# A causal convolution's tap products moved from VectorE to ScalarE and adding transfers, in a hybrid encoder block

## The chip, the cores and the metric

The kernel runs on one core of one Trainium2 chip. The metric is device microseconds of one execution on that core; three runs of a kernel are timed and the median counts. Engines are named TensorE (PE in the profile), VectorE (DVE), ScalarE (ACT), GpSimd (POOL) and SyncE (SP). SyncE does no arithmetic here and issues nearly all transfers.

## The reference, cut to what matters

One layer of an encoder block, 256 rows of 4096 float32 values, all in float32. A wide input projection gives the parts of two branches: 16 heads of chunked attention, and a convolution module on 2048 channels. The change touches the causal depthwise convolution of the second branch, with 31 taps:

```python
u = a * jax.nn.sigmoid(g)
u = jnp.pad(u, ((0, 0), (CONV_K - 1, 0), (0, 0)))
u = lax.conv_general_dilated(
    u, w_dw[:, None, :], window_strides=(1,), padding='VALID',
    dimension_numbers=('NWC', 'WIO', 'NWC'),
    feature_group_count=CONV_WIDTH) + b_dw
u = jax.nn.silu(layer_norm(u, ln_g, ln_b))
return u @ w_pw + b_pw
```

So for each channel, output row t is the bias plus the sum over k of `w_dw[k]` times `u[t + k - 30]`. What follows it (layer norm, a pointwise product, gates, an output projection, a gated embedding and a last norm) is the same in both kernels.

## The kernel before

Every large product runs on TensorE in three passes: each float32 weight tile `wt` is split into a high part `wh` (a cast on ScalarE, line 204) and a low part `wl` (a subtraction on VectorE, line 205), and each block of activations was split likewise. `wh` and `wl` have three buffers each, `wt` has five. A product covers two column blocks of 512 at once (`mixed_product`) in 16 units of two 128-row blocks. A plain unit takes two `wt` tiles and 24 matmuls of 128x512. A unit with a star in the order strings (`early`, `dense` and so on) uses seven products in place of eight: 21 matmuls, and it also casts two sums of weight blocks, `ua` and `ub` (into `uh` and `ul`). Weights come by transfers of 512 KB that SyncE issues.

The order in time is: input projection of the convolution's `a` and `g` for column blocks 0 and 1 (`glu_conv(0)`, `glu_conv(1)`), then queries and keys, values, attention, `glu_conv(2)`, `glu_conv(3)`, more keys and attention, the layer norm, and so on.

`glu_conv(c)` ends with `uT`, the gated input of 512 channels with channels on partitions: four channel blocks of 128 channels by 256 rows, in one tile 128x4x256. The convolution of these four blocks is then not issued at once. Its instructions go as small closures into a queue `later`, and each unit of the products that follow takes a given number of closures from it (`fill`, by the list `early_fills`: 64 for a product of 16 units). There are 124 closures for one `uT`, in all 496 for the four. A scheduler then decides where each instruction stands on its engine, and it may bring one forward; engines run their instructions in that order.

Before, each closure is one VectorE instruction: `conv_tap` for one channel block and one tap. The first writes `cv` as product plus bias (line 678), the other 30 add one shifted product into `cv` in place (line 682). The layer norm (`layer_norm_swish`) reads all four `cv` tiles after the last of them is done. `cv` lies in the pool `act`, which has eight buffers of 4 KB a partition.

GpSimd has little to do: fills of constants, four times a fill of a part of `bias` for the attention (line 901), and a few tiny powers.

Of the kernel before, what the change touches and what calls it, by code (L numbers as in the profile page):

```python
# [10 lines left out]
F32 = mybir.dt.float32  # L11
F32R = mybir.dt.float32r
AF = mybir.ActivationFunctionType
ALU = mybir.AluOpType
AX = mybir.AxisListType

P = 128
# [8 lines left out]
def hybrid_block(  # L26
# [23 lines left out]
    nc = tc.nc  # L50
    _, T, D = x.shape
# [5 lines left out]
    TAPS = w_dw.shape[1]  # L57
    PAD = TAPS - 1
# [9 lines left out]
    def pool(name, bufs, stack=ctx, side=0, **kw):  # L68
        return stack.enter_context(tc.tile_pool(name=name, bufs=bufs, side=sides[side], **kw))

    cpool = pool("cpool", 1)
    act = pool("act", 8)
# [13 lines left out]
    def tmp_psum():  # L86
        return ps_tmp.tile([P, 512], F32, tag="tmp", name="tmp_ps")
# [92 lines left out]
    later = deque()  # L180
# [300 lines left out]
    def scaled_pair(w, col, apart, order, r, fills, home={}, then=lambda: None, **kw):  # L481

        t, z = [], []

        def on_helpers(helper):
            for dst, src in zip((t, z), sum_tiles(**home)):
                dst.extend(src)
            then()
            nc.scalar.activation(z[0][0], helper["P1"], AF.Identity, scale=r[:, :1])
            helper_sums(helper, z)  # L490
            for h, j in QUARTERS[1:]:
                nc.scalar.activation(z[h][j], z[h][j], AF.Identity, scale=r[:, h : h + 1])

        c = mixed_product(w, col, xT, xS, order, on_helpers, fills=fills, apart=apart, **kw)
        for h, j in QUARTERS:
            stt(
                z[h][j], c[h][j], r[:, h : h + 1], z[h][j],
                ALU.mult, ALU.subtract if j else ALU.add,
            )
        return t  # L500
# [17 lines left out]
    for c in range(0, 4, 2):  # L518
        if c:
            t = upool.tile([P, 4, 2, T], F32R, tag="big", name="big_t", bufs=1)  # L520
        else:
            t = keep.tile([P, 4, 2, T], F32R, tag="comb", name="comb_t")
# [126 lines left out]
    ln_g, ln_b, bdw, ga, gc, gp = (prm[:, a : a + n] for a, (_, n) in zip(at, rows))  # L649
    dw = spool.tile([P, KCW, TAPS], F32, name="dw", bufs=1)  # L650
# [22 lines left out]

    conv = []

    def conv_tap(cv, uT, i, b, k):
        if k == PAD:
            nc.vector.tensor_scalar(
                cv[:, i, :], uT[:, i, :], dw[:, b, k : k + 1], bdw[:, b : b + 1], ALU.mult, ALU.add
            )  # L680
        else:
            nc.vector.scalar_tensor_tensor(  # L682
                cv[:, i, PAD - k :], uT[:, i, : T + k - PAD], dw[:, b, k : k + 1],
                cv[:, i, PAD - k :], ALU.mult, ALU.add,
            )

    def more_combinations(pair):

        if pair in (7, 9):
            c = (pair + 1) // 2  # L690
            xS[2 * c] = act.tile([P, 2, 2, T], F32R, tag="act", name="comb_x"), 0
            later.extendleft(reversed(combinations(c)))

    def glu_conv(c):
        if c == 0:
            sg, gate = scaled_pair(
                w_in0, o_a, o_g - o_a, first, r_x, (1,), begin=first_pairs
            )
        else:
            last = c == CW // NB - 1  # L700
            sg, gate = scaled_pair(
                w_in0, o_a + c * NB, o_g - o_a, early_six if last else early, r_x, early_fills,
                ahead=more_combinations if last else None,
            )
        for h in range(NH):
            nc.scalar.activation(gate[:, h, :], gate[:, h, :], AF.Sigmoid)
            tt(sg[:, h, :], sg[:, h, :], gate[:, h, :], ALU.mult)
        uT = spool.tile([P, 4, T], F32, tag="hd", name="uT", bufs=5)
        for pair in range(2):
            pt = tmp_psum()  # L710
            for i in range(2):
                for h in range(NH):
                    b = 2 * pair + i
                    nc.tensor.transpose(
                        pt[:, i * T + h * P : i * T + (h + 1) * P],
                        sg[:, h, b * P : (b + 1) * P],
                        ident,
                    )
            nc.scalar.copy(
                uT[:, 2 * pair : 2 * pair + 2, :], pt.rearrange("q (i t) -> q i t", t=T)  # L720
            )
        cv = act.tile([P, 4, T], F32, tag="act", name="cv")
        for i in range(4):
            for k in reversed(range(TAPS)):
                later.append(partial(conv_tap, cv, uT, i, 4 * c + i, k))
        conv.append(cv)


# [191 lines left out]
    n_g = H // GH  # L920
    assert n_g == CW // NB == 4
    glu_conv(0)
    glu_conv(1)
    load_bias(0)
    keys(0, early_fills)
    values(0, early, early_fills, home=dict(tag="hd", bufs=5))
    attention(0)
    glu_conv(2)
    glu_conv(3)
    load_bias(1)  # L930
# [139 lines left out]
    for c0 in range(0, D // NB, 2):  # L1070
        for j in range(2):
            hc = act.tile([P, NH, NB], F32, tag="act", name="hc")
            c = c0 + j
# [222 lines left out]
```

## Time and profile before

| | |
|---|---|
| three timed runs | 2048.33, 2048.42, 2051.77 us; median 2048.42 us |
| span of the profiled execution, first to last instruction | 2049.8 us |
| the profiled execution's own time | nothing beside its span is given; the span is 1.4 us above the median of the runs |
| TensorE busy | 2021.3 us, 99% of the span |
| VectorE busy | 1944.7 us, 95% |
| ScalarE busy | 1196.2 us, 58% |
| GpSimd busy | 8.1 us |
| transfers | 412.30 MB, mean 201 GB/s |

The page is one profiled execution. A busy share is an average over stages with different limits, and a matmul counts as busy from its start to its modelled end, so that neighbours overlap. "Idle before" of a group of instructions is the time that its engine stood still just before them, with what ended it.

### The profile page before, as it was taken

The page shows a single profiled execution, that of the slowest core. Times are in us where ns is not written, and L with a number is a line of the kernel's source. Part 1 is how long each engine was busy: PE and PEld are TensorE (multiplying, and loading weights), DVE is VectorE, ACT ScalarE, POOL GpSimd, SP SyncE. Part 2 cuts the span into 40 slices and gives each one's busy share as a digit, 9 for nine tenths or more (in the row PEclk, how much of TensorE's full clock was granted, in tenths as well). Part 3 has the DMA queues.
Part 4 walks back from the last instruction along what each step waited for, and adds up shares of the span by engine and source line. Part 5 has one row for each costly group of instructions (what it writes and reads, how often), then busy time and mean ns, then how long its engine had stood idle before and what let it go on. Part 6 is the DMA issues. An engine that isn't in the chain of part 4 may idle for free.

```text
span 2049.8 us, 26039 instructions
## 1 busy us (share of the span) xinstructions
PE 2021.3 (99%) x9082; PEld 1652.6 (81%) x9082; DVE 1944.7 (95%) x2784; ACT 1196.2 (58%) x1543; POOL 8.1 (0%) x19
## 2 busy tenths in 40 slices
PE   9999999999899999999999999999999999999997
PEld 7888888888678888877888888888888888888876
DVE  7999999989999999988899999999999999999998
ACT  7655545655555544576565656676565666655555
POOL 0000000000000000000000000000000000000000
PEclk9999999999999999999999999999999999999998
DMA  8666666566665665754666566676666656666765
GB/s 284 195 195 205 201 192 203 166 198 184 194 187 170 200 184 184 222 164 168 196 217 206 191 218 196 217 241 208 212 200 202 205 188 209 200 219 206 235 207 178
DMA packets 153662, 412.30 MB, mean 201 GB/s; under 512 B 12974, under 2 KB 16190, under 8 KB 153530
## 3 DMA queue, kind: packets, MB, share of 16 engines
q1 hardware_dynamic: 152880, 409.80, 62.7%
q8 instruction: 71, 1.16, 0.2%
q10 hardware_dynamic: 650, 0.84, 0.1%
q14 instruction: 61, 0.50, 0.1%
HBM read 406.39 MB, written 4.19 MB: 200 GB/s over the span
## 4 chain that ended last, share of the span: by engine, by line
PE 87%; DVE 8%; issue 2%; DMA 1%; ACT 1%; SPq 0%; POOL 0%; POOLq 0%; ACTq 0%; DVEq 0%
PE acc L372 68%; PE acc_P L372 15%; DVE wl L205 3%; DVE cv L682 1%; DVE ul L205 1%; PE tmp_ps L170 1%; DMA wt<-in_w_in_dram 1%; PE acc L218 1%; DVE ub L433 0%; DVE ub L432 0%; PE tmp_ps L835 0%; PE tmp_ps L851 0%; DVE ua L428 0%; PE tmp_ps L869 0%; DVE ua L429 0%
## 5 line engine op out<-in xcount | busy, mean ns | idle before, releaser
L372 PE MATMUL acc<-wh,big_t 128*128 128x512 f32 x4196 | 1296.4, 392 | 4.0 <-DVE wh L563 1.6
L204 ACT CAST wh<-wt 128x1024 fp32r<-128x1024 f32 (+1 forms) x737 | 711.9, 977 | 552.3 <-PE acc L372 408.0
L372 PEld LDWEIGHTS acc<-wh,big_t 128*128 128x128 f32 x4196 | 784.2, 188 | 168.5 <-ACT big_t L156 2.4
L205 DVE TENSOR_TENSOR wl<-wt,wh 128x1024 fp32r<-128x1024 f32 (+1 forms) x737 | 821.0, 1125 | 32.3 <-ACT wh L204 28.9
L372 PE MATMUL acc<-wl,big_t 128*128 128x512 f32 x2098 | 804.0, 391 | 2.0 <-DVE wl L205 1.8
L372 PEld LDWEIGHTS acc<-wl,big_t 128*128 128x128 f32 x2098 | 393.0, 188 | 87.1 <-DVE wl L205 5.7
L682 DVE SCALAR_TENSOR_TENSOR cv<-uT,dw,cv 128x255 f32<-128x255 f32 (+22 forms) x480 | 213.1, 463 | 1.0
L204 ACT CAST uh<-ub 128x1024 fp32r<-128x1024 f32 x130 | 136.9, 1053 | 125.5 <-DVE ub L433 105.1
L204 ACT CAST uh<-ua 128x1024 fp32r<-128x1024 f32 x130 | 137.1, 1054 | 84.9 <-DVE ua L429 79.6
L205 DVE TENSOR_TENSOR ul<-ub,uh 128x1024 fp32r<-128x1024 f32 x130 | 158.7, 1221 | 8.1 <-ACT uh L204 6.9
L372 PE MATMUL acc_P<-uh,big_t 128*128 128x512 f32 x528 | 161.7, 393 | 0.0
L205 DVE TENSOR_TENSOR ul<-ua,uh 128x1024 fp32r<-128x1024 f32 x130 | 158.6, 1220 | 0.9 <-ACT uh L204 0.2
L372 PEld LDWEIGHTS acc_P<-uh,big_t 128*128 128x128 f32 x528 | 97.4, 188 | 24.3 <-ACT uh L204 5.0
L428 DVE TENSOR_TENSOR ua<-wt 128x512 f32<-128x512 f32 x130 | 89.3, 687 | 21.8 <-DMA wt<-in_w_in_dram 15.0
L372 PE MATMUL acc_P<-ul,big_t 128*128 128x512 f32 x264 | 101.1, 394 | 1.0 <-DVE ul L205 1.0
L429 DVE TENSOR_TENSOR ua<-wt 128x512 f32<-128x512 f32 x130 | 89.1, 685 | 2.3 <-DMA wt<-in_w_in_dram 1.3
L433 DVE TENSOR_TENSOR ub<-ub,wt 128x512 f32<-128x512 f32 x130 | 89.1, 686 | 0.8
L432 DVE TENSOR_TENSOR ub<-ua,wt 128x512 f32<-128x512 f32 x130 | 89.1, 685 | 0.3
L372 PE MATMUL acc<-uh,big_t 128*128 128x512 f32 x260 | 80.6, 390 | 0.0
L372 PE MATMUL acc_P<-wh,big_t 128*128 128x512 f32 x260 | 80.6, 389 | 0.0
L372 PE MATMUL acc_P<-uh,comb_t 128*128 128x512 f32 x228 | 70.1, 392 | 0.2
L372 PEld LDWEIGHTS acc_P<-ul,big_t 128*128 128x128 f32 x264 | 49.2, 188 | 15.2 <-DVE ul L205 4.9
(240 smaller groups left out, 1367.4 us busy)
## 6 DMA issues: line engine op xcount, KB each, us to landing
wt<-in_w_in_dram SPq DMA_DIRECT2D x447, 512.0 KB, 4.2
wt<-in_w_out_dram SPq DMA_DIRECT2D x128, 512.0 KB, 4.2
wt<-in_w_ple_gate_dram SPq DMA_DIRECT2D x128, 512.0 KB, 4.1
wt<-in_w_pw_dram SPq DMA_DIRECT2D x32, 512.0 KB, 4.6
hc<-in_x_dram SPq DMA_DIRECT2D x8, 512.0 KB, 5.2
wt<-in_w_ple_dram SPq DMA_DIRECT2D x8, 512.0 KB, 4.7
xin<-in_x_dram SPq DMA_DIRECT2D x7, 512.0 KB, 7.9
out_dram<-hc SPq DMA_DIRECT2D x12, 256.0 KB, 2.4
```

What stands on the lines that cost most here:

```text
L170: nc.tensor.transpose(pt[:, i * T + h * P : i * T + (h + 1) * P], src[:, h, b] if len(src.shape) == 4 else src[:, h, b * P : (b + 1) * P], ...
L204: nc.scalar.copy(wh[:, :kc, :], wt[:, :kc, :]),
L205: nc.vector.tensor_tensor(wl[:, :kc, :], wt[:, :kc, :], wh[:, :kc, :].bitcast(F32), ALU.subtract),
L218: nc.tensor.matmul(acc, a, b[:, k, :], start=kb == 0 and kind == 0, stop=kb == kblocks - 1 and kind == 2,)
L372: nc.tensor.matmul(banks[name], a, b, start=name not in begun, stop=final and ends[name] == n and kind == 2 and not (left and name in "P2 ...
L428: plus(ua[:, 0], w0[:, 0], w0[:, 1])
L429: plus(ua[:, 1], w0[:, 1], w1[:, 1])
L432: plus(ub[:, 0], ua[:, 0], w1[:, 1])
L433: plus(ub[:, 1], ub[:, 0], w1[:, 0])
L682: nc.vector.scalar_tensor_tensor(cv[:, i, PAD - k :], uT[:, i, : T + k - PAD], dw[:, b, k : k + 1], cv[:, i, PAD - k :], ALU.mult, ALU.add,)
```

## The change

Each closure is now a ScalarE instruction. `conv_taps` makes them for one `uT`. Four closures (`start`) write `cv` as product plus bias, for tap 30, which needs no shift. Then, for each of the 30 other taps, four closures (`tap`) write the products of the four channel blocks into one tile `tap` of 128x4x256, shifted; the fourth also has GpSimd issue a transfer of that tile, 512 KB, that adds it into `cv`. Two `tap` tiles alternate, taken from the pool `act`; their first 30 columns, which no product with a shift reaches in full, are set to zero by GpSimd once for each of the two tiles. Taps run from the largest shift (k = 0) to the smallest. VectorE has no part in it any more. The number of closures is the same, 124 for one `uT`.

```diff
-    def conv_tap(cv, uT, i, b, k):
-        if k == PAD:
-            nc.vector.tensor_scalar(
-                cv[:, i, :], uT[:, i, :], dw[:, b, k : k + 1], bdw[:, b : b + 1], ALU.mult, ALU.add
-            )
-        else:
-            nc.vector.scalar_tensor_tensor(
-                cv[:, i, PAD - k :], uT[:, i, : T + k - PAD], dw[:, b, k : k + 1],
-                cv[:, i, PAD - k :], ALU.mult, ALU.add,
-            )
+    def conv_taps(cv, uT, c):
+
+        held = {}
+
+        def start(i):
+            b = 4 * c + i
+            nc.scalar.activation(
+                cv[:, i, :], uT[:, i, :], AF.Identity,
+                scale=dw[:, b, PAD : PAD + 1], bias=bdw[:, b : b + 1],
+            )
+
+        def tap(k, i):
+            if k < 2 and i == 0:
+                held[k] = act.tile([P, 4, T], F32, tag="act", name="tap")
+                nc.gpsimd.memset(held[k][:, :, :PAD], 0.0)
+            t, b = held[k % 2], 4 * c + i
+            nc.scalar.activation(
+                t[:, i, PAD - k :], uT[:, i, : T + k - PAD], AF.Identity,
+                scale=dw[:, b, k : k + 1],
+            )
+            if i == 3:
+                nc.gpsimd.dma_start(cv, t, accum_op=ALU.add)
+
+        yield from (partial(start, i) for i in range(4))
+        yield from (partial(tap, k, i) for k in range(PAD) for i in range(4))
...
         cv = act.tile([P, 4, T], F32, tag="act", name="cv")
-        for i in range(4):
-            for k in reversed(range(TAPS)):
-                later.append(partial(conv_tap, cv, uT, i, 4 * c + i, k))
+        later.extend(conv_taps(cv, uT, c))
         conv.append(cv)
```

In the changed kernel the product of a tap is line 692, its transfer line 697, the zero fill line 690 and the start line 682; lines after it are 13 higher than before.

The order of ScalarE's instructions, in the units of `glu_conv(1)`, before: casts of weights and of their sums stand one behind the other. What a row waits for stands in brackets (DMAHW: a transfer that SyncE issued, DMASW: one that GpSimd issued, PE, DVE, Pool, Activation: that engine).

```order
L204 CAST uh<-ua 128x1024 [waits DVE_49]
L204 CAST wh<-wt 128x1024 [waits DMAHW1_49,PE_49,Activation_49]
L204 CAST wh<-wt 128x1024 [waits DMAHW2_49,PE_49,Activation_49]
L204 CAST wh<-wt 128x1024 [waits DMAHW3_49,PE_49,Activation_49]
L204 CAST uh<-ub 128x1024 [waits DVE_49]
L204 CAST wh<-wt 128x512 [waits DMAHW4_49,PE_49,Activation_49]
L204 CAST wh<-wt 128x1024 [waits DMAHW5_49,DVE_49,PE_49]
```

The same place in the changed kernel, where the products of the taps for rows of 235 to 237 elements stand between the casts:

```order
L204 CAST uh<-ub 128x1024 [waits DVE_49,PE_49]
L692 ACTIVATE tap<-uT,dw 128x235 [waits Activation_49]
L204 CAST wh<-wt 128x1024 [waits DMAHW5_49,PE_49,Activation_49]
L692 ACTIVATE tap<-uT,dw 128x236 [waits DMASW0_49,Activation_49]
L692 ACTIVATE tap<-uT,dw 128x236 [waits Activation_49] x3
L204 CAST wh<-wt 128x1024 [waits DMAHW6_49,PE_49]
L204 CAST wh<-wt 128x1024 [waits DMAHW7_49,PE_49]
L692 ACTIVATE tap<-uT,dw 128x237 [waits DMASW1_49,Activation_49]
L204 CAST uh<-ua 128x1024 [waits DVE_49,PE_49]
```

Behind the casts nothing was taken away; the first product of each tap waits for a transfer of GpSimd, the one that read the same `tap` tile two taps earlier.

GpSimd's order before, from the power for the input norm to the last fill of `bias`:

```order
L139 TENSOR_TENSOR r_x<-r_x,mhalf 128x2 [waits DVE_49,Pool_49]
L901 MEMSET bias 64x4x64 [waits DMAHW3_49]
L901 MEMSET bias 64x4x64 [waits DMAHW5_49,DMAHW3_49,DMAHW7_49,DVE_49,PE_49]
L901 MEMSET bias 64x4x64 [waits DMAHW7_49,DVE_49,Pool_49]
L139 TENSOR_TENSOR r_ln<-r_ln,mhalf 128x2 [waits DVE_49]
L901 MEMSET bias 64x4x64 [waits DMAHW5_49,PE_49]
```

GpSimd's order now, from the 23rd transfer of the first `cv` to the first transfer of the second:

```order
L697 DMA cv<-tap 128x1024 [waits DMASW5_49,Activation_49]
L697 DMA cv<-tap 128x1024 [waits DMASW6_49,Activation_49]
L914 MEMSET bias 64x4x64 [waits DMAHW3_49]
L697 DMA cv<-tap 128x1024 [waits DMASW7_49,Activation_49]
L697 DMA cv<-tap 128x1024 [waits DMASW0_49,Activation_49]
L697 DMA cv<-tap 128x1024 [waits DMASW1_49,Activation_49]
L697 DMA cv<-tap 128x1024 [waits DMASW2_49,Activation_49]
L697 DMA cv<-tap 128x1024 [waits DMASW3_49,Activation_49]
L697 DMA cv<-tap 128x1024 [waits DMASW4_49,Activation_49]
L690 MEMSET tap 128x4x30 [waits DMAHW5_49,PE_49]
L690 MEMSET tap 128x4x30 [waits DMAHW2_49,PE_49]
L697 DMA cv<-tap 128x1024 [waits DMAHW7_49,Activation_49,Pool_49]
```

Each transfer waits for the one before it to land, since both add into the same `cv`, and 120 of them now stand on a queue that held a fill now and then.

## The prediction

> **What bounds the kernel now.** I read the page's head first, then the busy time by stretch, then who waits for whom.
>
> ```profile
> PE 2021.3 (99%) x9082; PEld 1652.6 (81%) x9082; DVE 1944.7 (95%) x2784; ACT 1196.2 (58%) x1543; POOL 8.1 (0%) x19
> ...
> L682 DVE SCALAR_TENSOR_TENSOR cv<-uT,dw,cv 128x255 f32<-128x255 f32 (+22 forms) x480 | 213.1, 463 | 1.0
> ```
>
> TensorE is busy 99% of the span and VectorE 95%; the 480 adding taps are 213 us of VectorE. The question is whether VectorE holds TensorE up where the taps run, 107 to 807 us, and what ScalarE has free there.
>
> ```profile
> core 0: us, PE busy (x) PEld busy (x) DVE busy (x) ACT busy (x) POOL busy (x), PEclk, DMA share, GB/s
> 107.00:807.00 700.00, 692.79 (x3100) 564.31 (x3099) 686.50 (x1089) 364.35 (x434) 0.61 (x2) 1.00 0.62 191
> ```
>
> VectorE is busy 686.5 of 700 us, yet TensorE stands still for only 700 - 692.8 = 7.2 us. So what VectorE does there is nearly all hidden behind matmuls, and 7.2 us is about the most that its relief can bring. ScalarE has 336 us free.
>
> ```profile
> ACT wh L204 <- PE acc L372: 213.3, 129, 4.4
> ```
>
> In the same 700 us ScalarE waits 213 us for TensorE to give back a `wh` buffer: its casts run ahead as far as three buffers allow. This lead is the cushion that a late ScalarE eats first.
>
> **Where the taps now stand.** ScalarE's order keeps the casts of line 204 in nearly the same sequence, so I count casts to place the new work in the old trace. For the first `uT` (block 0) the first tap product stands behind 40 such casts and the last behind 92; for blocks 1 to 3 it is 119 to 168, 200 to 262 and 283 to 331 (counted, up to two off where the stretches below are cut). In the trace of before these casts lie here:
>
> ```profile
> core 0: us, ACT busy (x), PEclk, DMA share, GB/s
> 0.00:106.75 106.75, 39.84 (x40) 1.00 0.73 236
> 106.75:217.22 110.47, 51.09 (x52) 1.00 0.65 201
> 217.22:277.02 59.80, 26.90 (x28) 1.00 0.61 191
> 277.02:387.65 110.62, 48.63 (x49) 1.00 0.62 190
> 387.65:456.56 68.91, 31.59 (x32) 1.00 0.63 197
> 456.56:586.16 129.60, 59.83 (x62) 1.00 0.61 187
> 586.16:635.13 48.97, 21.08 (x21) 1.00 0.60 185
> 635.13:747.18 112.05, 47.21 (x48) 1.00 0.60 184
> ```
>
> So the 120 tap products and 30 transfers of a block do not spread over 700 us: they are packed into four stretches of 110.5, 110.6, 129.6 and 112.1 us, 462.7 us in all, with 49 to 69 us between them in which no tap runs. All engines in these four:
>
> ```profile
> 106.75:217.22 110.47, 110.25 (x487) 89.68 (x486) 109.43 (x175) 56.19 (x61) 0.31 (x1) 1.00 0.65 201
> 277.02:387.65 110.62, 110.62 (x509) 91.28 (x508) 109.88 (x186) 60.31 (x83) 0.00 (x0) 1.00 0.62 190
> 456.56:586.16 129.60, 123.89 (x536) 98.39 (x535) 129.29 (x208) 66.30 (x73) 0.31 (x1) 1.00 0.61 187
> 635.13:747.18 112.05, 111.96 (x519) 91.88 (x518) 109.96 (x189) 58.77 (x82) 0.00 (x0) 1.00 0.60 184
> ```
>
> **VectorE's part removed.** 480 x 0.463 us, and 16 starts. It lay beside TensorE, which stood still 0.2, 0, 5.7 and 0.1 us in these stretches. I take 0 us: the 5.7 us of block 2 vanish into what the stretch becomes below. Both ends: 0 and 7.2 us gained.
>
> **ScalarE's part added.** 480 products and 16 starts. The nearest rows:
>
> ```profile
> L492 ACT ACTIVATE z<-z,r_x 128x512 f32<-128x512 f32 x30 | 20.6, 718 | 12.8 <-DVE z L471 11.1 <-DVE z L473 1.6
> L265 ACT CAST big_t<-comb 128x512 fp32r<-128x512 f32 x20 | 12.0, 616 | 2.6 <-DVE comb L260 2.2 <-issue 0.3
> L804 ACT CAST big_t<-cv 128x256 fp32r<-128x256 f32 x16 | 5.2, 403 | 0.0
> L794 ACT ACTIVATE cv<-cv,prm 128x256 f32<-128x256 f32 x16 | 8.4, 591 | 0.0
> 209.75 2.00 ACT L204 CAST wh<-wt 128x1024 fp32r<-128x1024 f32 x2 [0.70 <-PE acc L372]
> ```
>
> Line 492 is the same operation at 512 columns (scaled by a column, SBUF to SBUF): 0.718 us. The two casts give 616 - 403 = 213 ns for 256 columns, so a product of 256 columns takes 0.505 us and of the mean 240.5 columns 0.49 us. Two casts in a row take 2.00 us together, not 2 x 1.05, so instructions in a row overlap by some 0.1 us, and a product costs 0.40 to 0.49 us. A start is like line 794, 0.59 us. Per block: 120 x 0.40 to 0.49 = 48 to 59 us, plus 2.4. With the 56 to 66 us that ScalarE has there already it comes to 107 to 118, 111 to 122, 117 to 128 and 109 to 120 us, against 110.5, 110.6, 129.6 and 112.1: just full. I take it as hidden; at the upper end blocks 0, 1 and 3 run over by 7, 11 and 8 us.
>
> **The transfers.** 120 of them, 512 KB each. Each waits for the one before it in the same `cv`; the first product of tap k waits for the transfer of tap k - 2; behind this product stand the casts that TensorE needs. So a block takes at least 28 transfers in a row (those of taps 0 to 27) plus the first tap's and the last tap's products, 8 x 0.45 = 3.6 us, and the cushion gives something back: two `wh` tiles ahead, each of 12 matmuls at 110.62 / 509 = 0.217 us, 5.2 us. With D for one transfer from its issue to the next, a block takes 28 D - 1.6 us, and it is late by that less its stretch. The point from which it counts: D = 112 / 28 = 4.0 us for blocks 0, 1 and 3, and 4.7 for block 2.
>
> No adding transfer, none from GpSimd and none from SBUF to SBUF is in the trace. The nearest rows, size and time from issue to landing:
>
> ```profile
> wt<-in_w_in_dram SPq DMA_DIRECT2D x447, 512.0 KB, 4.2
> xin<-in_x_dram SPq DMA_DIRECT2D x7, 512.0 KB, 7.9
> gin_rows<-in_norm_in_g_dram SPq DMA_DIRECT2D x1, 16.0 KB, 2.0
> ...
> q1 hardware_dynamic: 152880, 409.80, 62.7%
> ```
>
> A plain load of this size, beside the other loads, takes 4.2 us; one of 16 KB, which moves nearly nothing, 2.0. So 2.0 is fixed and 2.2 is data. An adding transfer must read two blocks, `tap` and `cv`, and write one. Below, D is the plain 4.2 us; above, twice all of it, 8.4, close to the slowest row of the size, 7.9. I take the fixed part once and the data twice: D = 2.0 + 4.4 = 6.4 us. It is an estimate, and the whole sum hangs on it.
>
> The Trainium skill, page "DMA: Bandwidth & Descriptors", section "Anatomy of one DMA — SWDGE (gpsimd) path", gives a transfer that GpSimd issues 2.0 us plus its bytes over 436 GB/s: for 512 KB an estimate of 3.2 us, under 4.0, so that by it the transfers stay hidden and the time stays near 2048. The trace does not agree for SyncE's loads, 4.2 us beside other traffic, and shows nothing of GpSimd's.
>
> The sum: a block takes 28 x 6.4 - 1.6 = 177.6 us, four 710.4; less 462.7 is 247.7 us. By D = 4.2 a block takes 116.0: late by 5.5, 5.4, 0 and 3.9, +15 us. By 8.4, 233.6 x 4 - 462.7 = +472 us.
>
> Are the 16 transfer engines enough? 409.8 MB took 62.7% of 2049.8 us, so 512 KB take 1.64 us of all of them. Doubled, 120 take 394 us; the weights take 0.62 x 462.7 = 287. Together 681 of 710 us: it is the row of landings that ends a stretch, narrowly, and the loads will land later than 4.2 us.
>
> GpSimd's own: eight zero fills beside the four fills of `bias`, each 0.3 us, on an engine that is idle. The first fill of `bias` now stands behind 24 transfers; the attention that reads it has its exponentials behind tap 24 of block 1, a whole stretch later. If it were not covered, attention 0 would wait for block 0's transfers, which ScalarE waits for anyway: 0 us.
>
> ```profile
> L901 POOL MEMSET bias<- 64x256 f32 x4 | 1.2, 307 | 790.0 <-DMA bias<-in_rel_table_dram 440.0 <-DVE cv L682 350.0
> ```
>
> Span 2049.8 + 247.7 = 2297.5. The median of the runs is 1.4 us under the profiled span, so I predict 2296 us, 12% slower.
>
> **Rivals.** First, on the other side: an adding transfer goes from issue to issue in under 4.0 us, and ScalarE's products cost 0.40. Then no tap waits, and of the 7.2 us of TensorE's standstill up to all is won: 2041 to 2048 us. For it speaks that `tap` and `cv` need no HBM; against it the 4.2 us of a plain load and the second read.
>
> Second: the transfers are hidden, but ScalarE at 0.49 us is over full. Blocks 0, 1 and 3 run over by 7, 11 and 8 us, less 5.2 of cushion each: 2 + 6 + 3 = 11 us, 2060 us.
>
> Third: the waits slow TensorE's clock. A stretch of 178 us holds 111 us of matmuls, so TensorE stands still 38% of the time, in pieces.
>
> ```profile
> 520.00:530.00 10.00, 5.90 (x24) 3.86 (x23) 10.00 (x17) 5.77 (x7) 0.00 (x0) 1.00 0.39 109
> 2040.00:2045.00 5.00, 0.00 (x0) 0.00 (x0) 2.31 (x6) 2.56 (x4) 0.94 (x1) 0.50 0.48 179
> ```
>
> At 5.9 busy of 10 us the granted clock stayed 1.00; with no matmul in 5 us it was 0.50. At half clock the matmuls of a stretch take twice as long, 925 us for the four, which is +463: 2511 us. The Trainium skill, page "TensorE: Matmul & The Clock Gate", section "Part 1: The HAM clock gate (the "warmup" mystery)", has the clock halve after an idle window of some 3.4 us; by that, pieces of 2 to 3 us leave it full. The two rows agree, so I hold this rival for unlikely.
>
> **How the numbers follow.** Row of transfers with a full clock, D from 4.2 to 8.4 or a little over: 77 in 100. Hidden: 11, of which 5 faster by over 0.2% (about what a measurement of this kernel can tell from no change) and 6 within. ScalarE over full: 4. Clock halved: 8. Slower in all 77 + 4 + 8 = 89. The range reaches from 2070 (D = 4.3: 118.8 a block, late by 8.3, 8.2, 0 and 6.7, +23) to 2520 (D = 8.4), which leaves out the hidden cases, ScalarE alone and the far end of the clock's case, about 2 in 10.
>
> **What would show it.** Right: 120 transfers `cv<-tap` of 512 KB from GpSimd with 6 to 7 us from issue to landing; ScalarE's largest new wait is that of `tap`, line 692, for `cv<-tap`, some 250 us; the four stretches take about 178 us each, TensorE busy near 62% in them, its clock 1.00; VectorE far under 90%; the stretches between and all after 807 us unchanged in length. Wrong, if the transfers land in 4 us or less, if the tap products take other than 0.4 to 0.5 us, if a clock of 0.50 shows in the stretches, or if the loads of `wt`, not the taps, are what TensorE waits for.

## The result and the profile after

The changed kernel takes 2307.09 us (median of 4 runs, 2303.75 to 2309.3) against 2049.09 us for the kernel before: a ratio of 1.1257, 95% interval 1.1243 to 1.127. The profiled execution has a span of 2302.0 us, 252.2 us more than before's. The prediction was 2296 us, with a range of 2070 to 2520.

The head of the page after, the chain that ended last, the transfers' queue, the rows of the new work (busy time and mean ns of one, then the engine's idle time before it and its releasers), and the transfers' size and median time from issue to landing:

```profile
span 2302.0 us, 26473 instructions
...
PE 2114.4 (92%) x9082; PEld 1690.5 (73%) x9082; DVE 1774.2 (77%) x2288; ACT 1382.1 (60%) x2039; POOL 113.7 (5%) x147
...
q0 software_dynamic: 17280, 62.92, 14.9%
...
PE 51%; DMA 13%; issue 4%; DVE 3%; ACT 2%; POOL 0%; ACTq 0%; POOLq 0%; DVEq 0%
...
L692 ACT ACTIVATE tap<-uT,dw 128x226 f32<-128x226 f32 (+14 forms) x480 | 207.9, 487 | 278.8 <-DMA cv<-tap 278.7
...
L697 POOL DMA_DIRECT2D cv<-tap x120 | 104.2, 868 | 829.7 <-ACT tap L692 540.7
...
cv<-tap POOLq DMA_DIRECT2D x120, 512.0 KB, 5.2
```

VectorE's share fell from 95 to 77%, but TensorE's fell too, from 99 to 92%, and transfers now make up 13% of the span in the chain of work that ended last. Where they are seen is the view of one line: the transfers' own instructions, what GpSimd waited for ahead of them, and who waited for them.

```profile
L697 POOL DMA_DIRECT2D cv<-tap x120: 859/862/1042, 108.0 to 1001.2; - x120
...
  ACT tap L692: 540.7, 102
...
  ACT tap L692: 278.7, 107
...
DMA to landing us min/median/max: 4.5/5.2/9.5
```

The first of the two rows `ACT tap` is what GpSimd waited for, the second who waited for the transfers: ScalarE's products, 107 times, 278.7 us in all. The first names the wrong releaser. In all four blocks GpSimd issues the next transfer 0.64 us (median; least 0.53, and between 0.6 and 0.7 in 108 of 116 cases) after the landing of the one before, so it is the landing that lets it go.

The four blocks, each from the start of its first tap product to the start of its last (columns as in the windows of the prediction):

```profile
105.80:283.60 177.80, 133.29 (x485) 99.11 (x484) 78.89 (x85) 102.57 (x186) 25.63 (x30) 0.87 0.84 207
342.50:516.20 173.70, 135.65 (x531) 102.54 (x530) 84.43 (x108) 104.65 (x203) 25.16 (x29) 0.88 0.83 206
590.70:772.50 181.80, 144.21 (x528) 105.99 (x527) 97.78 (x112) 109.84 (x193) 25.46 (x30) 0.90 0.86 213
821.10:994.70 173.60, 138.00 (x539) 102.60 (x537) 85.92 (x107) 103.65 (x203) 24.98 (x29) 0.90 0.83 203
sum 706.90, PE 551.14 PEld 410.25 DVE 347.03 ACT 420.71 POOL 101.23; mean PE 137.79 PEld 102.56 DVE 86.76 ACT 105.18 POOL 25.31
```

They sum to 706.9 us and hold the 52, 49, 62 and 48 casts that the prediction counted; before, these took 462.7 us. The difference, 244.2 us, is nearly the whole loss. TensorE's matmuls have grown too, in the first block from 110.3 us for 487 of them to 133.3 us for 485, because the granted clock fell to 0.87 to 0.90 on average; that is a consequence, as the row of landings would end the stretch anyway.

### The profile page after: what moved, and what is told of

Its sections match the earlier page's. It is cut to its first block, busy times and chain, and to the rows that moved or that the text cites. A ratio compares the mean times of both kernels' runs of the same rounds, so it can differ in the third digit from the quotient of the medians.

```text
span 2302.0 us, 26473 instructions
## 1 busy us (share of the span) xinstructions
PE 2114.4 (92%) x9082; PEld 1690.5 (73%) x9082; DVE 1774.2 (77%) x2288; ACT 1382.1 (60%) x2039; POOL 113.7 (5%) x147
## 3 DMA queue, kind: packets, MB, share of 16 engines
q0 software_dynamic: 17280, 62.92, 14.9%
## 4 chain that ended last, share of the span: by engine, by line
PE 51%; DMA 13%; issue 4%; DVE 3%; ACT 2%; POOL 0%; ACTq 0%; POOLq 0%; DVEq 0%
PE acc L372 38%; DMA cv<-tap 12%; PE acc_P L372 11%; DVE wl L205 1%; ACT tap L692 1%; PE acc L218 1%; PE tmp_ps L170 1%; DMA wt<-in_w_out_dram 1%; DMA wt<-in_w_in_dram 0%; ACT wh L204 0%; DVE ul L205 0%; DVE ub L432 0%; DMA wt<-in_w_ple_dram 0%; ACT uh L204 0%; DVE ua L429 0%
## 5 line engine op out<-in xcount | busy, mean ns | idle before, releaser
L372 PE MATMUL acc<-wh,big_t 128*128 128x512 f32 x4196 | 1332.0, 400 | 92.1 <-ACT wh L204 88.5
L372 PEld LDWEIGHTS acc<-wh,big_t 128*128 128x128 f32 x4196 | 799.3, 192 | 276.9 <-ACT wh L204 109.6
L372 PE MATMUL acc<-wl,big_t 128*128 128x512 f32 x2098 | 831.5, 402 | 29.1 <-DVE wl L205 28.6
L372 PEld LDWEIGHTS acc<-wl,big_t 128*128 128x128 f32 x2098 | 401.9, 192 | 143.3 <-DVE wl L205 61.3
L692 ACT ACTIVATE tap<-uT,dw 128x226 f32<-128x226 f32 (+14 forms) x480 | 207.9, 487 | 278.8 <-DMA cv<-tap 278.7
L697 POOL DMA_DIRECT2D cv<-tap x120 | 104.2, 868 | 829.7 <-ACT tap L692 540.7
L372 PE MATMUL acc<-uh,big_t 128*128 128x512 f32 x260 | 86.0, 413 | 0.0
```

What stands on the lines that cost most here:

```text
L372: nc.tensor.matmul(banks[name], a, b, start=name not in begun, stop=final and ends[name] == n and kind == 2 and not (left and name in "P2 ...
L692: nc.scalar.activation(t[:, i, PAD - k :], uT[:, i, : T + k - PAD], AF.Identity, scale=dw[:, b, k : k + 1],)
L697: nc.gpsimd.dma_start(cv, t, accum_op=ALU.add)
```

## The experiments

**No transfer.** The two lines that issue the transfer are left out, so the tap products are made and never added:

```diff
-            if i == 3:
-                nc.gpsimd.dma_start(cv, t, accum_op=ALU.add)
```

> The products of all taps still run on ScalarE, but no transfer adds them into cv, so cv holds tap 30 and the bias alone. Theory (the row of adding transfers, each waiting for the landing of the one before, sets the length of the four stretches): without transfers the 252 us are gone, and the stretches go back from 178, 174, 182 and 174 us to about 110 to 130 each: 2043 to 2060 us. Rival, ScalarE over full with 480 products more: more than 2060 us, with TensorE waiting for casts in the stretches. If the 252 us come from elsewhere (order of the program, clock), the time stays near 2300.

Measured: 2041.25 us (2039.42 to 2042.5), ratio 0.9959 (0.9944 to 0.9973). The packed stretches without the transfers, as windows:

```profile
107.10:198.20 91.10, 90.18 (x402) 74.21 (x401) 63.61 (x68) 89.67 (x172) 0.79 (x4) 1.00 0.65 203
273.80:358.90 85.10, 85.10 (x382) 70.47 (x381) 61.73 (x68) 84.57 (x165) 0.00 (x0) 1.00 0.62 195
459.30:563.80 104.50, 103.07 (x457) 84.44 (x456) 84.78 (x99) 102.31 (x187) 0.51 (x2) 1.00 0.64 198
625.50:720.60 95.10, 95.10 (x448) 78.17 (x447) 70.37 (x93) 94.10 (x194) 0.00 (x0) 1.00 0.58 179
```

ScalarE is busy for 370.7 of these 375.8 us and TensorE still for 373.5: ScalarE is full, as predicted, and TensorE hardly waits for its casts (sum, times, longest from 100 to 1100 us):

```profile
PE acc L372 <- ACT wh L204: 0.4, 1, 0.4
```

So all of the 12.6% comes with the transfers, and the relief of VectorE alone is worth some 8 us (5.5 to 11.5 by the interval). This kernel is the base for what follows: over it the changed kernel spends 261.3 us of span.

**Plain copies.** The same transfers without the addition:

```diff
-                nc.gpsimd.dma_start(cv, t, accum_op=ALU.add)
+                nc.gpsimd.dma_start(cv, t)
```

> The same 120 transfers of 512 KB on the same queue with the same waits, but plain: each overwrites cv in place of adding to it. It leaves out the add and with it the second read. Theory: a packet of 4 KB of the adding transfer took 327 ns and one of the plain loads 159, so eight packets an engine are 1.34 us shorter; a transfer goes from issue to issue in about 4.7 us in place of 6.2, a block takes 28 x 4.7 + 3.6 = 135 us against stretches of 110.5, 110.6, 129.6 and 112.1: +77 us, about 2127 us. Rival, fixed part (issue on GpSimd, first packet, landing) rules: within 20 us of 2307. Rival, the add itself is cheap and it is waiting behind loads that makes it slow: also near 2300.

Measured: 2179.8 us (2178.49 to 2182.16), ratio 1.0637 (1.0621 to 1.0652), about half of the loss; the guess of 2127 was too low, because it counted 4.7 us for a transfer. The page's row of the transfers:

```profile
cv<-tap POOLq DMA_DIRECT2D x120, 512.0 KB, 4.2
```

From issue to issue a transfer takes 5.04 to 5.16 us in the four blocks, and the blocks 143.3, 148.9, 148.5 and 145.7 us, which is 28 x 5.1 + 3.6 = 146.4. The formula holds at a second value of D, without the cushion of 5.2 us.

**The transfers by themselves.** A kernel with nothing but rows of dependent transfers, 12 of each kind, and no other traffic.

> No part of the reference is computed and the output is zero: only rows of 12 transfers from SBUF to SBUF, each waiting for the one before, nothing beside them. From issue to next issue, theory (fixed part plus data, two reads for an add): adding from GpSimd 128 KB 3.1 us, 256 KB 3.8, 512 KB 5.15, 1 MB 7.9; plain from GpSimd 512 KB 3.8, 128 KB 2.8; plain from SyncE 512 KB 3.3. Rival, the add has no price of its own: adding and plain 512 KB alike. Rival, the loads beside it made the price: adding 512 KB well under 4.5 us to landing.

The answers for one line each: 256 KB, 512 KB and 1 MB adding, 512 KB and 128 KB plain, all from GpSimd.

```profile
L34 POOL DMA_DIRECT2D dst<-src x12: 860/864/886, 42.0 to 82.5; - x12
```

```profile
L36 POOL DMA_DIRECT2D dst<-src x12: 860/866/888, 86.2 to 140.3; - x12
...
DMA to landing us min/median/max: 4.5/4.5/4.6
```

```profile
L38 POOL DMA_DIRECT2D dst<-src x12: 860/866/886, 145.2 to 225.9; - x12
...
DMA to landing us min/median/max: 6.9/6.9/7.0
```

```profile
L40 POOL DMA_DIRECT2D dst<-src x12: 527/527/554, 233.2 to 268.9; - x12
...
DMA to landing us min/median/max: 2.8/2.8/3.2
```

```profile
L42 POOL DMA_DIRECT2D dst<-src x12: 536/536/545, 272.5 to 298.4; - x12
```

First and last start over 11 steps give the time from issue to issue: (140.3 - 86.2) / 11 = 4.92 us, (225.9 - 145.2) / 11 = 7.34 us, and 3.25 us for the plain copy of 512 KB, 2.35 us for that of 128 KB. Each 512 KB more of adding costs 2.42 us, so 512 KB alone cost 2.50 fixed and 2.42 for the data. Each 128 KB more of plain copy costs 0.90 / 3 = 0.30 us, so the plain 512 KB cost 2.06 fixed and 1.19 for the data: the data of an adding transfer cost twice a plain one's. Beside the weight loads the same adding transfer took 6.06 to 6.33 us from issue to issue, some 1.3 us more. Of these 0.25 us lie between the landing and the next issue (0.64 against 0.39 here); the rest, some 1.05 us, comes before the landing, beside the neighbours.

**Half chains.** Each tap is sent in two transfers of 256 KB, each waiting only for its own half of `cv`:

```diff
-            if i == 3:
-                nc.gpsimd.dma_start(cv, t, accum_op=ALU.add)
+            if i % 2:
+                h = slice(i - 1, i + 1)
+                nc.gpsimd.dma_start(cv[:, h], t[:, h], accum_op=ALU.add)
```

> The same bytes in 240 transfers of 256 KB: channel blocks 0 and 1 of a tap go as soon as their products are made, blocks 2 and 3 after theirs, so that two rows of transfers run beside each other, each waiting for its own last landing. Theory (latency of a row): the data of one row runs in the fixed part of the other, a tap takes 4.0 to 4.8 us in place of 6.2, a block 116 to 138 us: 2055 to 2135 us, about 2100. Rival, the 16 transfer engines are full: no change, about 2300. Rival, GpSimd's issue (0.87 us each, now 240): 52 us a block, no limit, so no change by it.

Measured: 2309.05 us (2306.8 to 2310.89), ratio 1.1267 (1.1248 to 1.1286): no change, where I expected 200 us back. The first two blocks as windows:

```profile
106.10:264.20 158.10, 116.50 (x427) 86.94 (x425) 65.60 (x70) 94.20 (x173) 50.80 (x59) 0.89 0.93 215
338.60:497.70 159.10, 111.95 (x404) 82.32 (x403) 66.47 (x75) 92.72 (x171) 50.34 (x58) 0.86 0.91 206
```

The blocks are shorter, 158 to 168 us (5.5 to 5.8 us a tap). But the scheduler also packed the taps into fewer casts, 43, 41, 55 and 41, so each block covers less other work. The four blocks sum to 644.7 us and the same casts take 378.6 us without transfers: late by 266.1 us; counted in this way, the changed kernel is late by 264 us. A transfer of 256 KB takes (82.5 - 42.0) / 11 = 3.68 us from issue to issue when it is alone, so with two rows beside the loads each row became slower. The 16 transfer engines, at 0.90 to 0.93 of their time in the four blocks, seem to leave little to win; that this is why the cost stayed the same is argued from their share, not tested by a run of its own.

**Fewer transfers.** VectorE takes back some taps and adds them into the tile on its way: 20, 15 or 10 transfers per block instead of 30. For 15, in short:

```diff
+            r, last = k % 2, k % 2 == 1
...
+            if r:
+                nc.vector.scalar_tensor_tensor(
+                    to, src, dw[:, b, k : k + 1], to, ALU.mult, ALU.add
+                )
+            else:
+                nc.scalar.activation(to, src, AF.Identity, scale=dw[:, b, k : k + 1])
+            if last and i == 3:
                 nc.gpsimd.dma_start(cv, t, accum_op=ALU.add)
```

> 20 transfers a block in place of 30: of each three taps ScalarE makes two products, in two tiles, and VectorE adds the third into the first of them before it goes. Theory (row of landings, about 6.1 us from issue to issue beside the loads): a block needs 18 x 6.1 + 3.6 = 113 us; by the count of casts in ScalarE's order the four stretches hold 95, 97, 126 and 105 us of work where no transfer holds it up: late by 18, 16, 0 and 8, +42 us over the 2041 without transfers, 2083 us, slower than before. Rival, the cost goes with the bytes or the number of transfers: two thirds of 266, 2041 + 177 = 2218 us.

> 15 transfers a block: of each two taps ScalarE makes one product and VectorE adds the other into the tile before it goes; VectorE keeps 240 of its 480 taps. Theory (row of landings): a block needs 13 x 6.1 + 3.6 = 83 us, and its stretches hold 90, 89, 124 and 93 us of other work: all hidden, and TensorE's 7 us of standstill mostly won: 2041 to 2047 us. Rival, the cost goes with the number of transfers: 2041 + 133 = 2174 us. Rival, the adding transfers hold up the loads of weights: over 2052 us, with VectorE and ScalarE waiting for wt.

> 10 transfers a block: of each three taps ScalarE makes one product and VectorE adds two into the tile before it goes; VectorE keeps 320 of its 480 taps. Theory (row of landings): 8 x 6.1 + 3.6 = 52 us a block, hidden with room: 2040 to 2046 us. Rival, the cost goes with the number of transfers: 2041 + 89 = 2130 us. Rival, VectorE still sets TensorE's standstill: 2046 to 2050, no change from before.

Measured: 2213.93 us (ratio 1.0807, 1.0789 to 1.0825), 2151.37 us (1.0507, 1.0489 to 1.0524) and 2101.95 us (1.0257, 1.0242 to 1.0272). All three expectations of my theory fell: by it a row of 20 landings costs some 42 us and rows of 15 and 10 hide. Over the kernel without transfers they cost 173, 110 and 61 us, so 2.2, 1.8 and 1.5 us for each transfer, and 2.2 in the changed kernel. This is nearer to the rival, a price for each transfer (2218, 2174 and 2130 us). The waits of the version with 15 show where, in the stretch that holds the taps:

```profile
POOL cv L701 <- DVE tap L695: 250.7, 17, 73.1
ACT tap L699 <- DMA cv<-tap: 170.5, 51, 7.5
```

GpSimd now mostly waits for VectorE's additions, and from a landing to the next issue it is 0.67 to 5.3 us (medians of the blocks), no longer 0.64: the row of landings does not set the pace. (With 20 the medians are still 0.64, so there it does in part.) But ScalarE still waits for a landing 51 times, 170.5 us, where tiles are refilled 52 times: the first product into a tile must wait until that tile's last contents are sent, and it stands in ScalarE's in-order queue ahead of the casts that TensorE needs, too early for a transfer of 6 us. A short row does not help where each transfer has such a wait of its own.

**Two transfers per block.** No tile is filled again after it was sent: two tiles, 15 taps each, 14 of them added by VectorE (`k % 15` in the diff above).

> Per block two tiles, each begun by one product per channel block on ScalarE and completed by 14 additions each on VectorE, then added to cv: two transfers per block, 8 in all, complete convolution. No tile is filled again after its transfer, so no product waits for a landing. New theory (price per refilled tile, about 2 us each: 112 of them in the changed kernel, 72, 52, 32 in the versions with 20, 15 and 10 transfers per block): 2046 to 2051, as before within what can be measured. Rival (1.5 to 2.2 us per transfer, refilled or not): 8 of them, 2058 to 2066.

Measured: 2048.97 us (2047.54 to 2051.14), ratio 0.9997 (0.9988 to 1.0006). The 8 transfers cost nothing that can be measured, though each takes 6.2 to 8.3 us to land:

```profile
  POOL tap L691: 10.8, 2
  DVE lnsum L773: 4.4, 1
...
DMA to landing us min/median/max: 6.2/6.6/8.3
```

Those two rows are all that waits for them, and no tap product is among them.

**The same traffic without the wait at the tile.** The transfers take `uT` instead of the tile, in the version with 20 and in the changed kernel; bytes, issues and the row into `cv` stay:

```diff
-                nc.gpsimd.dma_start(cv, t, accum_op=ALU.add)
+                nc.gpsimd.dma_start(cv, uT, accum_op=ALU.add)
```

> The kernel with 20 transfers per block (2213.9 us), but each adding transfer takes its 512 KB from uT, which is written once per block, and no longer from the tile that ScalarE fills next; the sums are therefore not the convolution's. Same 80 transfers, same bytes, same row of additions into cv (20 x 6.3 = 126 us per block, less than the 160 us from one block's start to the next), same products and same additions on VectorE; only no product has to wait until a tile has been sent away. New theory (the price of a transfer is ScalarE's wait for it at the refilled tile, 225 us in all in that kernel, which holds up the casts behind it): the time falls to 2041 to 2052, with the relief of VectorE two thirds of the 8.4 us seen without transfers. Rival (a transfer costs by its traffic or its issue, 2.2 us each, whoever waits): 2210 again. In between, say 2120: both.

> The changed kernel itself with one word altered: all 30 transfers of a block take uT, not the tile just filled; the sums are therefore not the convolution's. ScalarE's products wait for no landing. The four rows of 30 additions, 6.2 us each, still have to pass: about 4 x 186 = 744 us from 107 on, so up to 856, while without transfers the first reader of the sums (lnsum from cv) started at 724. New theory: the 265 us go except for what VectorE waits at that reader, 0 to 132 us: 2041 to 2173, with the blocks of products as short as without transfers (91 to 105 us). Rival (traffic or the row of landings itself takes the time): 2290 to 2310, blocks of 175 us.

Measured: 2167.15 us (2163.73 to 2168.42; ratio 1.0567, 1.055 to 1.0585) where I expected 2041 to 2052, and 2284.84 us (2284.39 to 2294.18; ratio 1.1156, 1.1134 to 1.1178) where I expected 2041 to 2173. Both missed. By the times alone the second would speak for the rival (2290 to 2310), and the first lies between the two. The waits of the second, from 100 to 1100 us, say more:

```profile
POOL cv L697 <- DMA cv<-uT: 633.0, 116, 8.9
...
ACT tap L692 <- POOL tap L690: 131.0, 2, 109.6
...
PE acc L372 <- ACT wh L204: 105.3, 1, 105.3
...
DVE ua L428 <- DMA wt<-in_w_in_dram: 73.6, 33, 5.1
DVE lnsum L769 <- DMA cv<-uT: 64.2, 1, 64.2
```

The waits of the tap products for landings are gone, and the first block takes 94.2 us where it took 177.8 (it holds 42 casts in place of 52). The row of landings moved to another queue: GpSimd waits 633.0 us for one transfer after the other, in order, and behind them stands line 690, the zero fill of the next block's tile. ScalarE's first product of that block waits 109.6 us for it, and TensorE 105.3 us for the cast behind; of block 3 it is another 21.4. Then the first reader of the sums, `lnsum` on VectorE, waits 64.2 us for the last of the four rows. These three make 195.2 of the 242.4 us of span over the kernel without transfers; where the other 47 us are stays open.

**The queue freed.** One word: the zero fill goes to VectorE. First in the version with 20 from `uT`, then with 15 from `uT`.

```diff
-                nc.gpsimd.memset(held[n][:, :, :PAD], 0.0)
+                nc.vector.memset(held[n][:, :, :PAD], 0.0)
```

> The kernel with 20 transfers per block taken from uT (2167.2 us), with one word altered: the memset of a new tile's first columns is done by VectorE instead of GpSimd (again not the convolution's sums). There, in the profile, ScalarE's first product of the second block waited 61.0 us for that memset, which stood on GpSimd's in-order queue behind adding transfers that each waited for the one before. Theory (the 124.8 us over the kernel without transfers are 61.0 for that, 23.0 for VectorE at the first reader of cv, and about 40 spread over the blocks): the 61 go, and 2041 + 40 + 23 to 35 at the reader (the last block now starts some 60 us earlier, so its row of additions is not farther ahead) = 2100, within 2085 to 2125. Rival (the transfers themselves cost it, and the wait only takes it up): 2160 to 2170.

> 15 transfers per block, from uT, memset on VectorE; otherwise the kernel with 15 transfers per block (2151.4 us), whose products have to wait for the tile to be sent away. Again not the convolution's sums. Theory: neither a product nor a memset waits for a landing, and four rows of 15 additions, 15 x 6.5 = 98 us each, end at about 625 + 98 = 723, when the first reader of the sums starts; left are VectorE's half of the relief (2041 + 4 = 2045) and the spread part, which was 40 us for 80 transfers, so 30 for 60: 2075, within 2045 to 2090. Rival (1.8 us per transfer, whoever waits): 2150.

Measured: 2117.21 us (2112.53 to 2121.69; ratio 1.0328, 1.031 to 1.0346) and 2079.62 us (2074.14 to 2085.45; 1.0147, 1.0121 to 1.0172). Both lie in the ranges of the theory. With 20, 76 us over the kernel without transfers are left, 23.2 of them VectorE's wait at the first reader of the sums. With 15, no product waits for a landing or for a zero fill; of the 110 us that 15 transfers cost, 38 are left. Part of them shows at the loads; transfers from 107 to 720 us, first without transfers, then with 15:

```profile
wt<-in_w_in_dram SPq DMA_DIRECT2D x222, 512.0 KB, 3.9
```

```profile
wt<-in_w_in_dram SPq DMA_DIRECT2D x210, 512.0 KB, 4.8
cv<-uT POOLq DMA_DIRECT2D x55, 512.0 KB, 6.5
```

A weight load lands 0.9 us later beside the transfers. TensorE's waits for VectorE's low parts, from 100 to 1100 us, grew too; first without transfers, then with 15:

```profile
PE acc L372 <- DVE wl L205: 1.1, 3, 0.6
```

```profile
PE acc L372 <- DVE wl L205: 25.1, 20, 3.4
```

VectorE's additions into the tile came in as well, so the 38 us are not divided between them and the later loads.

## Why the prediction was right, point by point

**The row of landings.** Right, and in each block: 28 x 6.2 + 3.6 = 177.2 us against 177.8, 173.7, 181.8 and 173.6 measured, and 177.6 predicted. That this is "transfer waits for transfer, product for transfer, casts behind the product" is shown: without transfers all is gone, with plain copies the block follows the shorter D, and with another source the first block, which nothing else disturbs, shrinks to 94.2 us (and the row reappears on GpSimd).

**D.** Right in the sum, 6.4 against 6.06 to 6.33, not in its sizes. From issue to landing it is 5.55 us on average, not 6 to 7; 0.64 us to the next issue come on top. The fixed part once and the data twice is right for a transfer alone: 2.42 against 1.19 us of data. But I took 2.0 fixed and twice 2.2 for the data, from loads beside other traffic. Alone it is 2.50 fixed and 2.42 for the data, and 1.3 us come on top beside the loads. Data 2.0 us too dear, against a fixed part 0.5 too small and 1.3 left out, came to nearly the same sum: that is luck. An adding transfer of 512 KB did not cost twice the plain one's whole: 4.92 against 3.25 us alone. The estimate of 3.2 us by the Trainium skill's page "DMA: Bandwidth & Descriptors", section "Anatomy of one DMA — SWDGE (gpsimd) path", agrees with the plain copy alone (2.8 to landing, 3.25 from issue to issue), not with the adding one, so its case, transfers hidden, was rightly a rival.

**The cushion.** Wrong: the 5.2 us were not given back; block lengths fit without them, in two kernels. A D that was 0.2 too high (28 x 0.2 = 5.6) happened to make up for it.

**Where it counts from.** Wrong, and hidden by this change's size. I had transfers free up to D = 4.0 us, as long as the row fits its stretch. The versions with 15 and 10 have rows that fit and lose 110 and 61 us; the one with 20 loses 173 us where its row explains some 42. The step that failed is "late by that less its stretch": it holds where the row of landings ends a block. Where it does not, ScalarE's wait at each refilled tile, one by one, is still paid.

**ScalarE's products.** Right: 0.487 us of mean for one, and 207.9 us busy for 480, so 0.433 us each with their overlap, inside 0.40 to 0.49, and hidden. The second rival, ScalarE over full, is refuted by the kernel without transfers: it is full and the kernel is faster.

**VectorE's relief.** Taken as 0, between 0 and 7.2. It is 8.4 us where nothing waits for a transfer (2049.68 less 2041.25, medians of the same runs; 5.5 to 11.5 by the interval), so near the upper end, which the measurement does not exclude; which us these are stays open. In the changed kernel the row of landings is longer than the relieved stretch, and nothing of it is seen.

**The clock.** I had 1.00 or half. It was 0.87 to 0.90, the mean of stretches at 1.00 and pieces at 0.50, and a 0.50 in the blocks was one of my signs of being wrong. In this trace the granted clock changes only on a grid of 3.41 us: from its fall at 125.66 us on, all its changes lie whole multiples of 3.413 us apart. Some pieces of this grid in block 0 (TensorE busy, granted clock, DMA share, GB/s):

```profile
193.93:197.34 3.41, 1.36 (x6) 1.00 0.68 201
197.34:200.75 3.41, 1.19 (x2) 0.50 0.81 154
200.75:204.17 3.42, 3.38 (x9) 0.50 0.64 171
204.17:207.58 3.41, 3.41 (x15) 1.00 0.97 178
207.58:211.00 3.42, 0.82 (x3) 1.00 0.58 168
211.00:214.41 3.41, 3.41 (x8) 0.50 0.95 214
214.41:217.82 3.41, 3.41 (x16) 1.00 0.92 237
```

TensorE stood still from 195.3 to 199.6 us, and the clock fell 2.05 us into this pause, at 197.34. It fell again at 211.00, after a pause from 207.7 to 209.8, when matmuls were running again. Both times the piece before held little work, 1.36 and 0.82 us of matmuls. Over the whole trace, with the profile's modelled ends of matmuls, each piece at full clock with TensorE busy for less than 0.47 of it was followed by 0.50, and none with more than 0.56 was; of those at 0.50, each with more than 0.89 was followed by 1.00, and none with less than 0.80. So in this trace it is the busy share of the piece before that goes with the clock, not the length of one pause. My reading that pauses of 2 to 3 us leave it full is wrong, and there are longer ones. TensorE's waits for a cast from 100 to 720 us (sum, times, longest):

```profile
PE acc L372 <- ACT wh L204: 63.2, 25, 6.3
```

The Trainium skill's page "TensorE: Matmul & The Clock Gate", section "Part 1: The HAM clock gate (the "warmup" mystery)", has the clock halve after an idle window of some 3.4 us; the trace agrees with the length of 3.4 us, but not with a window that has to be idle, as the clock fell 2.05 us into the pause of 4.27 us and after one of 2.08 us. The clock did not decide the time, as the row of landings is longer than the slowed matmuls, 133.3 of 177.8 us. It is also why TensorE's share in the blocks was 75 to 79%, not 62.

**The rest.** The 16 transfer engines came to 0.83 to 0.86, below the 681 of 710 us of the sum (the 120 transfers took 14.9% of 2302 us, 343 us, not 394), and only half chains brought them to 0.90 to 0.93. The three stretches between the blocks took 59.0, 74.5 and 48.6 us against 59.8, 68.9 and 49.0, and all after the last block 1307.3 against 1302.6. Nothing waited for GpSimd's fills of `bias`, so 0 us was right.

## What to carry to other kernels

Transfers that add into one buffer form a row, and the row must be costed as a row: its length by issue to issue beside the real traffic, and then the first in-order engine that waits for it, which may be the one that refills the source, the one that issues (everything behind it on that queue waits too), or the reader of the sum. Shortening the row is not enough: each refill of a sent buffer is a wait of its own, at the place in the engine's order that the scheduler chose. Work that ends in two transfers per block, with no refill, cost nothing here, but it moved too little work to gain anything; none of the versions that add up all taps was faster than the kernel before.

## What the runs showed of the hardware that I had not expected

- Issuing an adding transfer holds GpSimd for 0.86 us, a plain one 0.53 us.
- An adding transfer's data cost 2.42 us for 512 KB, and its fixed part 2.50 us, with nothing else running; for a plain copy it was 1.19 and 2.06 us.
- The granted clock changed on a grid of 3.41 us. It fell to 0.50 after each piece with TensorE busy for less than 0.47 of it, and came back after each with more than 0.89.
